# A two-layer hybrid decoder on one core: recurrent stage partly from PSUM, fewer early modulation rows, and a reordered start

## The chip, the core and the metric

The kernel runs on one core of a Trainium2 chip. The metric is the device time of one execution in microseconds (us). TensorE (PE in the profile; PEld is its weight load) multiplies matrices into eight PSUM banks; VectorE (DVE) and ScalarE (ACT) work on SBUF and PSUM; SyncE (SP) issues most of the DMA transfers, ScalarE a few.

## The reference

Two layers, 256 tokens, model width 1024. Each layer runs a half-step SwiGLU FFN, a token mixer and a second half-step FFN. The mixer of layer 0 is stick-breaking attention, that of layer 1 the Griffin RG-LRU block. Each sub-layer is RMS-normalised and takes shift, scale and gate from a conditioning vector c:

```python
mod = (c_act @ mod_w[layer] + mod_b[layer]).reshape(B, N_SUB, 3, D_MODEL)
h = rmsnorm(x, g) * (1 + scale) + shift          # sublayer_input
x = x + w * (1 + gate) * sublayer(h)

def rglru_block(h, ...):                         # D_RNN = 1280, ten blocks of 128
    gate, xb = jnp.split(h @ w_in, 2, axis=-1)
    xc = conv_b + sum of four taps of xb (a causal convolution of width 4)
    r = sigmoid(block-diagonal w_r @ xc + b_r)
    i = sigmoid(block-diagonal w_i @ xc + b_i)
    log_a = -8 * r * softplus(-lam); a = exp(log_a)
    b = sqrt(-expm1(2 * log_a)) * (i * xc)
    hs = linear recurrence h_t = a_t * h_(t-1) + b_t
    return (gelu(gate) * hs) @ w_out
```

The trunk ends with one RMSNorm.

## The kernel before

All activations lie transposed in SBUF: x is eight tiles of 128 features by 256 tokens. The weights come from HBM in float32. A chunk (`raw`) is split on the chip into a high part `wh` (ScalarE copies it to fp32r, L526) and a low part `wl` (VectorE subtracts, L529), and the activations likewise (`hx`, `arenar`). A product is then three fp32r passes on TensorE (L555): high by high, high by low, low by high. A few products run in plain float32 instead, without a split: the first chunk of the first FFN (L824), the block-diagonal gates of the recurrence (L1163), the sums of squares (L632), and the first down chunk of the recurrent stage (L572; `N32 = 1`).

The order of the work is not written by hand. Each step is recorded as an operation with an engine, a cost, its inputs and outputs; `Program.schedule` plans all of them with costs and due times (`LAT`, `START`, `SAME`), and the instructions of each engine are emitted in the planned order, which the engine then keeps. PSUM banks, weight buffers and work areas are handed out in that plan (`Buf`, `Space`).

The places that the change touches:

- `first_loads`: SP's queue loads c (`cb`), then x in two halves, then, one after the other, modulation rows and weights; ScalarE's queue loads the first parameters (`pars`). VectorE and ScalarE square x, VectorE adds the squares in pairs (L1317), and four float32 products with a matrix of ones (L632) sum them over the partitions. TensorE also runs filler products on zeros (`warm`, L1284): 4, 4 and then 18 ahead of the first real product (L824). `gbias` (L1298) is a small step on the parameters; the first modulation scales (`mf`) need it.
- `hook` and `rate`: a row of the modulation (128 outputs) is one 512 KB load and one multiply-and-sum on VectorE (L587). `rate[phase]` says how many rows are taken at each position of a phase, and `due[phase]` how many must be done near its end. Phase 0 is the first FFN, 1 attention, 2 and 3 the next two FFNs.
- `rglru`: TensorE projects xb (five pairs of 128-feature tiles); ScalarE copies a pair's halves from the bank to SBUF (`xb`); VectorE runs the four taps (`conv`, L1142 and L1145); `gates(n)` makes two float32 products per tile (L1163), two sigmoids and a tanh on ScalarE, and a product on VectorE (L1174). After the last sigmoid come, over all pairs, exponentials and squares (ScalarE) with L1220 (VectorE), square roots (ScalarE) with L1226, and the scans (L1229). Meanwhile TensorE runs the gate projections (`gate_proj`), which ScalarE copies out of their banks. Then a Gelu on ScalarE, the product y (L1236), its split (L1242), and the down projection (`down`) with five chunks of `wout`.
- Between two stages stands `residual` (x is updated, L702) and `scaled` (L650), which prepares the next stage's input.

Of the kernel before, what the change touches and what calls it, by code (L numbers as in the profile page):

```python
# [10 lines left out]
AF = mybir.ActivationFunctionType  # L11
# [358 lines left out]
def trunk(ctx, tc, xT, cb, par, modw, gu0, gu, wdn, qk, wv, wo, win, wri, wout, out):  # L370
# [111 lines left out]
    def col(off, n=1):  # L482
        return pars()[:, off : off + n]
# [644 lines left out]
    def rglru(l, s, nxt):  # L1128
        N32 = 1
        R, F = new_phase(8 * (NB - N32), 86)  # L1130
        xc, rr, th, gt, sig, wg, firsts = {}, {}, {}, {}, [], {}, []
# [3 lines left out]

        def conv(n, evict):
            xb = Buf(xbr)
            evict(n % 2, xb)
            if n % 2 == 0:
                xc[n // 2] = Buf(F, 4)  # L1140
            c, e, cs = of(xc, n)
            V(lambda: dve.tensor_scalar(c()[:, cs], xb()[:, 1 : 1 + T], col(OFF_CW + n), col(OFF_CB + n), ALU.mult,  # L1142
                                        ALU.add), T, [xb, pars], [(c, e)], ptr=2)
            for tap in range(1, 4):
                V(lambda tap=tap: dve.scalar_tensor_tensor(c()[:, cs], xb()[:, 1 + tap : 1 + tap + T],  # L1145
                                                           col(OFF_CW + tap * NR + n), c()[:, cs], ALU.mult, ALU.add), T,
                  [xb, pars, (c, e)], [(c, e)], ptr=1)

# [27 lines left out]
        def xb_proj(n2):  # L1176
            if n2 == 0:
                firsts.append(up_first((l, s), [load(win[1, i], CH, f"xb{i}") for i in range(NFIRST)]))
            if n2 < NFIRST:
                ts = next(firsts[0])  # L1180

                def evict(e, xb):
                    t, rd, c = ts[e]
                    A(lambda: xb()[:, 4:], t, AF.Identity, T, [t, rd], [xb], ptr=1, bias=c)
            else:
# [6 lines left out]
            for e in range(2):  # L1192
                conv(2 * n2 + e, evict)

        def gate_proj(n2):
            acc = Acc(f"gt{n2}")
            up(acc, load(win[0, n2], CH, f"gt{n2}"), (l, s), True)
            b = acc.b
            g = gt[n2] = Buf(F, 4)
            A(g, b, AF.Copy, 2 * T, [(b, (0, 0)), (b, (1, 0))], [g], psum=True)  # L1200

        for n2 in range(NB):
            xb_proj(n2)
            if n2 >= 2:
                gates(2 * n2 - 4)
                gates(2 * n2 - 3)
        gate_proj(0)
        for n in range(6, NR):
            gates(n)
        exps, sqs, ys = [], [], []  # L1210

        def decay(n2):
            r, t, q = rr[n2], th[n2], Buf(F, 4)
            for e in range(2):
                n, cs = 2 * n2 + e, slice(e * T, (e + 1) * T)
                exps.append(A(lambda cs=cs: r()[:, cs], lambda cs=cs: r()[:, cs], AF.Exp, T, [(r, e), nsp], [(r, e)],
                              table="exp", ptr=1, scale=lambda n=n: nsp()[:, n : n + 1], after=sig))
            A(q, r, AF.Square, 2 * T, [(r, 0), (r, 1)], [q])
            tt = [(t, 0), (t, 1)]
            V(lambda: dve.scalar_tensor_tensor(t(), q(), 1.0, t(), ALU.add, ALU.mult), 2 * T, [q] + tt, tt)  # L1220

        def scan(n2):
# [4 lines left out]
            for e in range(2):  # L1227
                cs = slice(e * T, (e + 1) * T)
                V(lambda cs=cs: dve.tensor_tensor_scan(t()[:, cs], r()[:, cs], c()[:, cs], 0.0, ALU.mult, ALU.add), T,  # L1229
                  [(c, e), (r, e)], [(t, e)])  # L1230

        def output(n2):
            g, t = gt[n2], th[n2]
            A(g, g, AF.Gelu_apprx_tanh, 2 * T, [g], [g], table="gelu", after=sqs)
            tt = [(t, 0), (t, 1)]
            V(lambda: dve.tensor_tensor(t(), t(), g(), ALU.mult), 2 * T, tt + [g], tt)  # L1236
            if n2 < N32:
# [49 lines left out]
    def first_loads(F):  # L1287
        c, b, halves = Buf(modr), [Buf(banks), Buf(banks)], []
        act_dma(lambda: pars()[:, :NP0], par[:, :NP0], [], [(pars, 0)])
        last[:] = [pr.op("DMA", 1000.0, lambda: sp.dma_start(c()[:1, :], cb), [], [c], last, lat=-900.0)]  # L1290
        warm(EARLY)
        for h in range(2):
# [4 lines left out]
        warm(MID, [pr.last_pe])  # L1297
        V(lambda: dve.scalar_tensor_tensor(gbias(), col(OFF_MB + KD, KD), 1.0, col(OFF_NG, KD), ALU.add, ALU.mult), KD,  # L1298
          [(pars, 0)], [gbias])


        pairs = []
        for h, scalar_ in enumerate(((0,), (2, 3))):
# [9 lines left out]
            for i in scalar_:  # L1313
# [100 lines left out]
```

## Time and profile before

| | us |
|---|---|
| three runs: lowest, median, highest | 959.68, 960.46, 961.25 |
| the profiled execution | 961.03 |
| its span, first to last instruction | 959.3 |
| TensorE busy | 948.8 |
| VectorE busy | 789.0 |
| ScalarE busy | 567.5 |

The profile shows one execution; its rows give the engine, the line of the kernel, the tiles written and read, the number of instructions and their time. Matmuls are pipelined, so the time of one row is longer than the distance from one to the next. A float32 product stands there as two rows. The TensorE clock that the throttle granted was 0.997 of full over the span.

### The profile page before, as it was taken

The numbers are of one execution on the slowest core, as the hardware profiler recorded it, in microseconds if no ns is written. First come the engines' busy times: TensorE is split into PE (matmuls) and PEld (weight loads), VectorE is DVE, ScalarE is ACT, GpSimd is POOL, SyncE is SP. The second block draws the span as 40 slices with busy tenths as digits, with TensorE's granted clock in tenths as the row PEclk, the third lists the DMA queues.
The fourth block names the chain that finished last, engine by engine and source line by source line (L and its number), as shares of the span: only waits on it lengthen the run. The fifth ranks groups of instructions, "written<-read, shape, count | busy, mean of one in ns | idle before, by whom it ended". The sixth has DMA issues, their size and how long they took to land.

```text
span 959.3 us, 19706 instructions
## 1 busy us (share of the span) xinstructions
PE 948.8 (99%) x8120; PEld 936.3 (98%) x8120; DVE 789.0 (82%) x1287; ACT 567.5 (59%) x925; POOL 2.4 (0%) x15
## 2 busy tenths in 40 slices
PE   9999999999999999999999999999999999999996
PEld 6999999999999999999999999999999999999996
DVE  7999988799999999888899989845997996555443
ACT  6685453379786765444466555534879785445333
POOL 1000000000000000000000000000000000000000
PEclk9999999999999999999999999999999999999998
DMA  9989999946766499889976899965243746555531
GB/s 347 405 307 373 351 353 353 334 190 249 255 222 220 180 347 366 332 297 348 363 260 255 312 345 364 355 212 198 88 173 136 264 164 235 210 182 197 169 119 44
DMA packets 48044, 251.25 MB, mean 262 GB/s; under 512 B 5457, under 2 KB 6097, under 8 KB 28242
## 3 DMA queue, kind: packets, MB, share of 16 engines
q1 hardware_dynamic: 47378, 249.43, 70.6%
q8 instruction: 63, 1.03, 0.4%
q10 hardware_dynamic: 576, 0.56, 0.2%
q14 instruction: 27, 0.22, 0.1%
HBM read 248.92 MB, written 1.05 MB: 261 GB/s over the span
## 4 chain that ended last, share of the span: by engine, by line
PE 83%; DVE 8%; ACT 3%; DMA 3%; issue 1%; SPq 0%; DVEq 0%; ACTq 0%
PE bank L555 76%; DVE wl L529 3%; DMA rawm<-in_modw 3%; PE bank L938 2%; DVE arenaf L1145 1%; PE bank L1068 1%; DVE rawm L587 1%; ACT wh L526 1%; ACT arenaf L502 1%; PE bank L572 1%; PE bank L824 1%; PE bank L632 1%; PE bank L1011 1%; DVE x L702 1%; ACT hx L502 1%
## 5 line engine op out<-in xcount | busy, mean ns | idle before, releaser
L555 PE MATMUL bank<-hx,wh 128*128 128x256 f32 (+1 forms) x3204 | 553.1, 277 | 0.8 <-DVE hx L650 0.8
L526 ACT ACTIVATE wh<-raw 128x1024 fp32r<-128x1024 f32 (+1 forms) x324 | 334.0, 1052 | 278.4 <-PE bank L555 210.1
L555 PEld LDWEIGHTS bank<-hx,wh 128*128 128x128 f32 x3204 | 485.0, 188 | 1.3 <-DVE hx L650 1.0
L529 DVE TENSOR_TENSOR wl<-raw,wh 128x1024 fp32r<-128x1024 f32 (+1 forms) x324 | 386.5, 1215 | 115.5 <-ACT wh L526 114.2
L555 PE MATMUL bank<-hx,wl 128*128 128x256 f32 (+1 forms) x1602 | 443.4, 277 | 0.0
L555 PEld LDWEIGHTS bank<-hx,wl 128*128 128x128 f32 x1602 | 301.3, 188 | 0.0
L555 PE MATMUL bank<-arenar,wh 128*128 128x256 f32 x1664 | 284.5, 277 | 0.0
L555 PEld LDWEIGHTS bank<-arenar,wh 128*128 128x128 f32 x1664 | 250.6, 188 | 0.1
L555 PE MATMUL bank<-arenar,wl 128*128 128x256 f32 x832 | 229.7, 276 | 0.0
L587 DVE SCALAR_TENSOR_TENSOR rawm<-rawm,cact 128x1024 f32<-128x1024 f32 x128 | 154.9, 1219 | 15.1 <-DMA rawm<-in_modw 15.1
L555 PEld LDWEIGHTS bank<-arenar,wl 128*128 128x128 f32 x832 | 156.2, 188 | 0.0
L502 ACT ACTIVATE arenar<-a 128x256 fp32r<-128x256 f32 x88 | 35.4, 406 | 11.5 <-DVE a L780 11.3
L502 ACT ACTIVATE sg<-bank 128x256 f32<-128x256 f32 x82 | 30.2, 370 | 17.3 <-PE bank L555 16.5
L785 DVE TENSOR_TENSOR arenar<-a,arenar 128x256 fp32r<-128x256 f32 x88 | 36.5, 419 | 0.5 <-ACT arenar L502 0.5
L780 DVE TENSOR_TENSOR a<-bank,sg 128x256 f32<-128x256 f32 x82 | 34.2, 418 | 1.8 <-ACT sg L502 1.5
L502 ACT ACTIVATE hx<-x,mf 128x256 fp32r<-128x256 f32 x40 | 18.6, 501 | 22.1 <-DVE x L702 22.0
L555 PE MATMUL bank<-hk,wh 128*128 128x256 f32 x156 | 30.3, 287 | 0.0
L702 DVE SCALAR_TENSOR_TENSOR x<-bank,mf,x 128x256 f32<-128x256 f32 x48 | 21.6, 479 | 7.7 <-PE bank L555 7.6
L938 PE MATMUL bank<-wh,hx 128*128 128x256 f32 x128 | 24.4, 285 | 0.2 <-DVE arenar L1076 0.2
L555 PEld LDWEIGHTS bank<-hk,wh 128*128 128x128 f32 x156 | 24.0, 188 | 0.3
L502 ACT ACTIVATE hx<-hpre,mf 128x256 fp32r<-128x256 f32 x41 | 19.7, 499 | 6.2 <-DVE hpre L658 6.1
L555 PE MATMUL bank<-hk,wl 128*128 128x256 f32 x78 | 21.9, 281 | 0.0
(118 smaller groups left out, 587.2 us busy)
## 6 DMA issues: line engine op xcount, KB each, us to landing
raw<-in_gu SPq DMA_DIRECT2D x79, 1024.0 KB, 5.7
rawm<-in_modw SPq DMA_DIRECT2D x128, 512.0 KB, 6.9
raw<-in_wdn SPq DMA_DIRECT2D x44, 1024.0 KB, 5.1
raw<-in_win SPq DMA_DIRECT2D x10, 1024.0 KB, 4.8
arenar<-in_modw SPq DMA_DIRECT2D x16, 512.0 KB, 9.2
raw<-in_qk SPq DMA_DIRECT2D x8, 1024.0 KB, 4.9
raw<-in_gu SPq DMA_DIRECT2D x14, 512.0 KB, 9.2
raw<-in_wout SPq DMA_DIRECT2D x5, 1024.0 KB, 5.0
```

Of the source, the lines that this page charges most:

```text
L502: act.activation(o(), i(), f, **{k: (v() if callable(v) else v) for k, v in kw.items()})
L526: act.activation(h()[:, :m], raw()[:, a : a + m], AF.Copy)
L529: dve.tensor_tensor(lo()[:, :m], raw()[:, a : a + m], f32(h()[:, :m]), ALU.subtract)
L555: pe.matmul(o(b()), wc(u()), xc(v()), start=start and n == 0, stop=stop and n == len(passes) - 1, skip_group_check=True)
L572: pr.op("PE", c_mm(n, 4), lambda: pe.matmul(o(b()), wc(w()), xc(x32()), start=start, stop=stop, skip_group_check=True), [w, x32] + ([] if ...
L587: dve.scalar_tensor_tensor(raw(), raw(), 1.0, cact(), ALU.mult, ALU.mult, accum_out=m()[:, t : t + 1])
L632: pr.op("PE", c_mm(T, 4), lambda i=i, q=q, c=c: pe.matmul(b()[:, :T], ones, q()[:, c], start=i == 0, stop=i == len(qs) - 1), [q] + [b] * ( ...
L702: dve.scalar_tensor_tensor(x[d](), acc.b()[:, j * T : (j + 1) * T], gate()[:, d : d + 1], x[d](), ALU.mult, ALU.add)
L780: V(lambda: dve.tensor_tensor(a(), b()[:, T:], sg(), ALU.mult), T, [(b, (1, 0)), sg], [a])
L785: V(lambda: dve.tensor_tensor(y[1](), a(), f32(y[0]()), ALU.subtract), n, [a, y[0]], [y[1]])
L824: pr.op("PE", c_mm(T, 4), lambda: pe.matmul(b()[:, g * T : (g + 1) * T], raw()[:, c0 : c0 + P], h0(), start=start, stop=False, skip_group_ ...
L938: pe.matmul(o, u()[:, tb * P : (tb + 1) * P], v()[:, c0 : c0 + 256], start=start and n == 0, stop=k == KD - 1 and n == 2, skip_group_check ...
```

## The change

In `first_loads` the load of c goes to ScalarE's queue, ahead of the parameters, so that x is first on SP's; the second group of squares is folded once more (three products with ones instead of four); `gbias` is planned behind that fold. The planner's start value for the DMA queue is 2900 instead of 2300.

Phase 0 takes 1.25 modulation rows per position instead of 1.5; phase 1 looks at its due number from position 8 instead of 9.

In `rglru` the last three pairs of xb stay in their PSUM bank: ScalarE computes the last tap with the bias from the bank (instead of the copy), and VectorE the other three taps from the bank, each on the columns that have a predecessor. The first two pairs are convolved on VectorE as before. The gates run three pairs behind the projection instead of two. The last two gate projections (`KEEP = 2`) stay in their banks until the Gelu reads them there. The squares of the first two pairs go to VectorE. `N32 = 0`: no down chunk is in float32; the first chunk's weights and the first pair's y are split like the others. The planner's cost of a scan is 600 ns.

```diff
-START = {"PE": 1170.0, "DVE": 2840.0, "ACT": 1960.0, "DMA": 2300.0}
+START = {"PE": 1170.0, "DVE": 2840.0, "ACT": 1960.0, "DMA": 2900.0}
...
-        N32 = 1
-        R, F = new_phase(8 * (NB - N32), 86)
+        N32 = 0
+        KEEP, TAPACT, SQACT = 2, False, (2, 3, 4)
+        R, F = new_phase(8 * (NB - N32), 86 - 4 * KEEP)
...
+            if acc is None:
+                xb = Buf(xbr)
+                evict(n % 2, xb)
+                src, rd, own = (lambda a, m: xb()[:, 4 - a : 4 - a + m]), [xb], True
+            else:
+                b, o = acc.b, (n % 2) * T
+                src, rd, own = (lambda a, m: b()[:, o : o + m]), [(b, (n % 2, 0))], False
+            if TAPACT or acc is not None:
+                A(lambda: c()[:, cs], lambda: src(0, T), AF.Identity, T, rd + [pars], [(c, e)], ptr=2, psum=acc is not None,
+                  scale=lambda: col(OFF_CW + 3 * NR + n), bias=lambda: col(OFF_CB + n))
+            else:
+                V(lambda: dve.tensor_scalar(c()[:, cs], src(0, T), col(OFF_CW + 3 * NR + n), col(OFF_CB + n), ALU.mult,
+                                            ALU.add), T, rd + [pars], [(c, e)], ptr=2)
+            for tap in range(3):
+                back = 3 - tap
+                z = 0 if own else back
+                def fn(tap=tap, back=back, z=z):
+                    u = c()[:, e * T + z : (e + 1) * T]
+                    dve.scalar_tensor_tensor(u, src(back, T - z), col(OFF_CW + tap * NR + n), u, ALU.mult, ALU.add)
+                V(fn, T, rd + [pars, (c, e)], [(c, e)], ptr=1)
...
-                def evict(e, xb):
-                    A(lambda: xb()[:, 4:], lambda: acc.b()[:, e * T : (e + 1) * T], AF.Copy, T, [(acc.b, (e, 0))], [xb],
-                      psum=True)
+                for e in range(2):
+                    conv(2 * n2 + e, acc=acc)
...
+            if n2 >= NB - KEEP:
+                gt[n2] = b
+                return
...
-            if n2 >= 2:
-                gates(2 * n2 - 4)
-                gates(2 * n2 - 3)
+            if n2 >= 3:
+                gates(2 * n2 - 6)
+                gates(2 * n2 - 5)
         gate_proj(0)
-        for n in range(6, NR):
+        for n in range(4, NR):
...
-            A(q, r, AF.Square, 2 * T, [(r, 0), (r, 1)], [q])
+            if n2 in SQACT:
+                A(q, r, AF.Square, 2 * T, [(r, 0), (r, 1)], [q])
+            else:
+                V(lambda: dve.tensor_tensor(q(), r(), r(), ALU.mult), 2 * T, [(r, 0), (r, 1)], [q])
...
-                  [(c, e), (r, e)], [(t, e)])
+                  [(c, e), (r, e)], [(t, e)], 600.0)
...
-            A(g, g, AF.Gelu_apprx_tanh, 2 * T, [g], [g], table="gelu", after=sqs)
+            if n2 >= NB - KEEP:
+                b, g = g, rr[n2]
+                rg = [(g, 0), (g, 1)]
+                A(g, b, AF.Gelu_apprx_tanh, 2 * T, [(b, (0, 0)), (b, (1, 0))], rg, table="gelu", psum=True, after=sqs)
+            else:
+                rg = [g]
+                A(g, g, AF.Gelu_apprx_tanh, 2 * T, [g], [g], table="gelu", after=sqs)
...
-        act_dma(lambda: pars()[:, :NP0], par[:, :NP0], [], [(pars, 0)])
-        last[:] = [pr.op("DMA", 1000.0, lambda: sp.dma_start(c()[:1, :], cb), [], [c], last, lat=-900.0)]
+        act_dma(lambda: c()[:1, :], cb, [], [c], 300.0)
+        act_dma(lambda: pars()[:, :NP0], par[:, :NP0], [], [(pars, 0)], 4800.0)
...
-            pairs += [(p, slice(0, T)), (p, slice(T, 2 * T))]
+            if h == 0:
+                pairs += [(p, slice(0, T)), (p, slice(T, 2 * T))]
+            else:
+                one = Buf(F, 2)
+                fold = V(lambda p=p: dve.tensor_tensor(one(), p()[:, :T], p()[:, T:], ALU.add), T, [p], [one])
+                pairs.append((one, slice(0, T)))
+        pr.op("DVE", 80.0, lambda: dve.scalar_tensor_tensor(gbias(), col(OFF_MB + KD, KD), 1.0, col(OFF_NG, KD), ALU.add,
+                                                            ALU.mult), [(pars, 0)], [gbias], [fold])
...
-    rate = {0: (1.5, SQ, 30), 1: (1.5, 0, 9), 2: (1.3, 0, 32), 3: (1.3, 0, 32)}
+    rate = {0: (1.25, SQ, 30), 1: (1.5, 0, 8), 2: (1.3, 0, 32), 3: (1.3, 0, 32)}
```

More of the change, by code (lines that the diff above doesn't have):

```diff
@@ L1141, in conv @@
             c, e, cs = of(xc, n)
[L1142 to L1147, printed above, removed]
+            if acc is None:
[18 more added lines that the diff above has]
+                V(fn, T, rd + [pars, (c, e)], [(c, e)], ptr=1)
         def gates(n):
@@ L1184, in evict @@
                     A(lambda: xb()[:, 4:], t, AF.Identity, T, [t, rd], [xb], ptr=1, bias=c)
+                for e in range(2):
+                    conv(2 * n2 + e, evict)
             else:
@@ L1187, in xb_proj @@
                 up(acc, load(win[1, n2], CH, f"xb{n2}"), (l, s), True)
-                def evict(e, xb):
-                    A(lambda: xb()[:, 4:], lambda: acc.b()[:, e * T : (e + 1) * T], AF.Copy, T, [(acc.b, (e, 0))], [xb],
-                      psum=True)
-            for e in range(2):
-                conv(2 * n2 + e, evict)
+                for e in range(2):
+                    conv(2 * n2 + e, acc=acc)
         def gate_proj(n2):
@@ L1297, in first_loads @@
         warm(MID, [pr.last_pe])
-        V(lambda: dve.scalar_tensor_tensor(gbias(), col(OFF_MB + KD, KD), 1.0, col(OFF_NG, KD), ALU.add, ALU.mult), KD,
-          [(pars, 0)], [gbias])
         pairs = []
```

6 lines of the change are left out of this document (2 added, 4 removed).

## The prediction

> **What bounds the kernel now.** I read the page first, then the table of waits of TensorE (who waited for whom, us in total, times, longest), then the chain that ended last.
>
> ```profile
> PE 948.8 (99%) x8120; PEld 936.3 (98%) x8120; DVE 789.0 (82%) x1287; ACT 567.5 (59%) x925; POOL 2.4 (0%) x15
> ...
> PE bank L555 <- DVE hx L650: 0.8, 1, 0.8
> PE bank L572 <- DVE arenaf L1236: 0.4, 1, 0.4
> PE bank L632 <- DVE arenaf L1317: 0.4, 1, 0.4
> ...
> 13.86 6.91 PE bank L824 x32
> 54.23 81.86 PE bank L555 x720
> 740.33 7.17 PE bank L572 x32
> ```
>
> TensorE is busy 948.8 of 959.3 us and its largest single waits are 0.8, 0.4 and 0.4 us. So time can be won in three ways only: fewer passes, an earlier first real product, or one of these waits. The chain gives the price of a pass. One fp32r pass takes 81.86/720 = 0.1137 us. A float32 product is recorded as two rows, and 32 rows take 6.91 us, so one product takes 2 x 0.216 = 0.432 us; the three fp32r passes that replace it take 0.341 us. VectorE or ScalarE work that is saved counts only where TensorE waits for it.
>
> **Part 1, the first microseconds.** Rows of the timeline: start, us, engine and line.
>
> ```profile
> 0.79 0.35 SPq L1290 DMA_DIRECT2D rawm<-in_cb  x1
> 1.20 0.82 SPq L495 DMA_DIRECT2D x<-in_xT  x2
> ...
> 3.30 0.16 DVE L1298 SCALAR_TENSOR_TENSOR gbias<-pars 128x8 f32<-128x8 f32 x1
> 5.78 0.96 DVE L1311 TENSOR_TENSOR arenaf<-x 128x768 f32<-128x768 f32 x1 [2.32 <-DMA x<-in_xT]
> 7.59 3.78 PE L632 MATMUL bank<-arenaf,ones 128*128 128x256 f32 x8 [0.40 <-DVE arenaf L1317]
> 8.24 0.69 DVE L1317 TENSOR_TENSOR arenaf<-arenaf 128x512 f32<-128x512 f32 x1
> 8.85 1.22 DVE L587 SCALAR_TENSOR_TENSOR arenar<-arenar,cact 128x1024 f32<-128x1024 f32 x1
> 10.00 1.22 DVE L587 SCALAR_TENSOR_TENSOR arenar<-arenar,cact 128x1024 f32<-128x1024 f32 x1
> 10.12 0.39 ACT L502 ACTIVATE mf<-mr,gbias,pars 128x1 f32<-128x1 f32 x1 [1.02 <-DVE arenar L587]
> 11.17 2.69 PE L1284 MATMUL bank<-zero 128*128 128x256 bf16 x18
> 12.43 0.48 DVE L658 SCALAR_TENSOR_TENSOR hpre<-x,mf,rst 128x256 f32<-128x256 f32 x1 [1.21 <-ACT rst L502]
> 13.01 0.51 ACT L502 ACTIVATE hpre<-hpre,mf 128x256 f32<-128x256 f32 x1 [0.43 <-DVE hpre L658]
> 13.70 7.07 PE L824 MATMUL bank<-hpre,raw 128*128 128x256 f32 x32
> ```
>
> VectorE waits 2.32 us for x. The load of c stands ahead of x on SP's queue and holds it from 0.79 to 1.20. With c on ScalarE's queue, x and every load behind it on SP start 0.41 us earlier. The bound below is 0, if x's slow arrival (issued 1.20, used 5.78) has another cause; I take 0.41, as the issue time is a plain shift. c is first on its new queue, and the parameters, now second there, are next read only behind the fold.
>
> Then, each row shifted by 0.41: the last L1317 ends at 8.52. The added fold, half as wide, lies between 0.35 (half of 0.69) and 0.48 (the 256-wide L658); with 0.45 it ends near 9.0. The two L587, 1.15 apart, end at 11.3; gbias, moved behind them in VectorE's order, adds its 0.16; mf 0.39 on ScalarE follows; L658 and the ScalarE step behind it (0.51) end near 13.05, where before they ended at 13.52. So the move of gbias eats most of what the fold gives, because mf now waits for it.
>
> On TensorE the eight L632 rows last from 7.59 to 11.17, 0.45 each. Six rows, the last two behind the fold, end near 9.9 instead of 11.17. But 18 filler matmuls (L1284) stand between them and L824.
>
> ```profile
> L632 PE MATMUL bank<-ssq,ones x12: 378/379/483, 202.5 to 950.5; 128*128 128x256 f32 x12
> L632 PE MATMUL bank<-arenaf,ones x8: 634/634/796, 7.6 to 10.7; 128*128 128x256 f32 x8
> ```
>
> The same L632 row (min/median/max ns) takes 634 ns here and 379 later: TensorE starts at a slow rate and reaches the full one only within the fillers, whose mean is 2.69/18 = 0.149 us. If that switch stays at its time and the fillers start 1.27 us earlier, 1.27 us more of slow time falls on them; at half rate that is 0.64 us of lost work, so they end at 9.9 + 2.69 + 0.64 = 13.2. L824 starts at 13.1 to 13.2 instead of 13.70: 0.55 us won. Ends of the range: 0 (no shift of x and the switch late) to 1.2 (the switch early, and mf not late). [...]
>
> **Part 2, fewer early modulation rows.** The rate 1.25 gives 36 rows (29 positions x 1.25) in place of 43 by the end of the first FFN. All 36 are used by the same date as before: 24 are due there, and 49 by the end of attention, where 48 are due, so nothing becomes late. But the 0.8 us wait at its end does not hang on their number:
>
> ```profile
> 200.01 1.22 DVE L529 TENSOR_TENSOR wl<-raw,wh 128x1024 fp32r<-128x1024 f32 x1
> 201.15 0.48 DVE L650 SCALAR_TENSOR_TENSOR hx<-x,mf,hx 128x256 fp32r<-128x256 f32 x1
> ```
>
> The last L650, for which TensorE waits, stands behind a weight split L529. In the instruction order of the changed kernel VectorE's and ScalarE's last steps before that point are the same, one modulation row among them. I take 0; at most 0.8 is won. The seven rows done later fall into FFNs where TensorE has no wait. Attention's TensorE order is the same but for six passes, so 0, within 0.5 either way.
>
> **Part 3, the recurrent stage: TensorE.** With N32 = 0 the 16 float32 products of the first down chunk become 48 fp32r passes: 16 x (0.432 - 0.341) = 1.46 us saved, with no cover needed. The chunk's weights must now be split: two wh on ScalarE, two wl on VectorE, and y of the first pair needs a hi copy and a lo subtraction. The gates of the first tiles run one projection later, in fewer blocks; this changes the order, not the number of passes.
>
> **Part 4, the recurrent stage: VectorE and ScalarE.**
>
> ```profile
> L702 DVE SCALAR_TENSOR_TENSOR x<-bank,mf,x x48: 474/478/485, 189.8 to 950.5; 128x256 f32<-128x256 f32 x48
> L1145 DVE SCALAR_TENSOR_TENSOR arenaf<-xb,pars,arenaf x30: 476/480/487, 690.1 to 712.7; 128x256 f32<-128x256 f32 x30
> ...
> ACT sg L502 <- DVE arenaf L1174: 1.5, 2, 1.0
> ...
> 723.99 0.48 ACT L502 ACTIVATE sg<-bank,pars 128x256 f32<-128x256 f32 x1
> 729.81 2.70 ACT L502 ACTIVATE arenaf<-arenaf 128x512 f32<-128x512 f32 x5
> 733.82 2.72 ACT L502 ACTIVATE arenaf<-arenaf 128x512 f32<-128x512 f32 x5
> 738.85 1.05 ACT L526 ACTIVATE wh<-raw 128x1024 fp32r<-128x1024 f32 x1
> 743.23 0.63 ACT L502 ACTIVATE arenar<-arenaf 128x512 fp32r<-128x512 f32 x1 [0.43 <-DVE arenaf L1236]
> ...
> 734.49 0.69 DVE L1226 TENSOR_TENSOR arenaf<-arenaf 128x512 f32<-128x512 f32 x1 [0.94 <-ACT arenaf L502]
> 735.21 1.27 DVE L1229 TENSOR_TENSOR_SCAN arenaf<-arenaf 128x256 f32<-128x256 f32 x2
> 736.41 0.67 DVE L1226 TENSOR_TENSOR arenaf<-arenaf 128x512 f32<-128x512 f32 x1
> 739.61 0.67 DVE L1236 TENSOR_TENSOR arenaf<-arenaf 128x512 f32<-128x512 f32 x1
> 743.11 2.36 DVE L529 TENSOR_TENSOR wl<-raw,wh 128x1024 fp32r<-128x1024 f32 x2
> 755.55 0.68 DVE L1242 TENSOR_TENSOR arenar<-arenaf,arenar 128x512 fp32r<-128x512 f32 x1
> ```
>
> Reading PSUM costs VectorE nothing: L702 reads a bank in 478 ns, the tap L1145 reads SBUF in 480. Six of the ten tiles lose their first tap on VectorE (ScalarE does it in place of the copy it did anyway). [...]
>
> Now the chain to the first down product. In before ScalarE ends the gates at 724.47, having waited 1.5 us for VectorE (sg, L1174). VectorE's lighter load and the new order take away most of that; I take 1.25 us (between 0 and 1.5). Two of the five squares go to VectorE, 2 x 0.54 us off ScalarE; but two wh of the new chunk, 0.95 us apart, stand ahead of the square roots. The roots start at 733.82 - 1.25 - 1.08 + 1.9 = 733.4, the first L1226 at 734.1, and its two pairs of scans end near 737.9. The roots (2.72), a table load and a Gelu let y of the first pair start at 738.1 and end at 738.75. ScalarE's hi copy (0.63) is done at 739.55, the lo subtraction at 740.2. Before, TensorE started at 740.33; now its first pass can start when it is ready and the second near 740.25: 0.2 us won.
>
> Then VectorE, to the last lo: 16 steps of 0.60 (L1229: two in 1.20) and 8 wl of 1.14 are 18.7 us, with gaps 759.2; before it was done at 756.23. TensorE asks for it after three chunks and 21 passes, (144 + 21) x 0.1137 = 18.8 us after 740.15, at 758.9: it waits 0.35 us. ScalarE's copies for two gate tiles (0.58 each) fall away; they stood on no path.
>
> **The sum.** -0.55 - 1.46 - 0.2 + 0.35 = -1.86 us. The profiled execution took 961.03 us around its span of 959.3 us, which makes 959.2; it lies 0.57 above the median of 960.46, so the median becomes 958.6.
>
> **The rivals.**
> *More is won* (chance 0.25): the wait for the last lo does not appear, and the start wins 1.2. For it: the sum of 18.7 us is within 0.4 of what is allowed. Against it: mf waits for gbias. Then -1.46 - 0.4 - 1.2 = -3.1, 957.4 us.
> *Only the passes are won* (0.15): the fillers run slow for longer and L824 stays near 13.6; the square-root chain keeps its old time, and y's split adds its 1.2 us to it, of which 0.2 to 0.4 is covered. Then -1.46 - 0.1 + 0.9 = -0.7, 959.8 us.
> *The recurrent tail becomes the bound* (0.10): ScalarE's sigmoids of all six late tiles come after one projection, behind banks that VectorE reads in strict order; two wh and three squares then stand in front of the roots. If the gates end at 728, 4 us later than before, the last lo comes 5.2 us later than in my sum and TensorE waits that long: -1.86 + 5.2 = +3.3, 963.8 us. It is slower than before from 1.9 us of such lateness over my sum, and over 0.2% slower from 3.8. Against it: VectorE has fewer steps ahead of the gates. [...]
>
> **How the numbers follow.** My own case has 0.50, and ranges from 957.6 to 959.5 by the ends of the start (0 to 1.2) and the waits of the tail (0 to 1). A change of 0.2% (1.9 us) is about what a measurement of this kernel can tell; 958.54 is that border, so half of my case lies on each side. Faster: 0.25 + 0.25 = 0.50; same: 0.25 + 0.15 = 0.40; slower: 0.10. The range of 8 in 10 runs from 956.9 to 960.7.
>
> **What would show it.** L572 is gone; L824 starts near 13.15; the wait for L650 near 200 us is still 0.8; the first down pass of the recurrent stage starts near 739.7 and TensorE loses some 0.4 us in its second, then some 0.35 about 19 us later; taps from a bank take 480 ns. I am wrong if the gates' last sigmoid ends after 724.5, if taps from PSUM take 540 ns, or if a new wait stands in attention.

## The result, and the profile after

The changed kernel takes **957.9 us** (median of 9 runs, 957.37 to 958.23) where the kernel before takes 960.26 in the same comparison (9 runs, 959.42 to 961.25). The ratio is 0.9978, with a 95% interval from 0.9969 to 0.9987: 1.2 to 3.0 us, or 2.1 by the ratio. The forecast was 958.6, within 956.9 to 960.7. The profiled execution took 957.58 us, its span is 955.8.

The page's first part and the table of waits of TensorE after (waited for: us in total, times, longest):

```profile
PE 946.8 (99%) x8134; PEld 935.1 (98%) x8134; DVE 793.0 (83%) x1287; ACT 568.2 (59%) x924; POOL 2.4 (0%) x15
...
PE bank L938 <- DVE arenar L1076: 0.2, 1, 0.2
PE bank L824 <- ACT hpre L502: 0.2, 1, 0.2
PE bank L632 <- ACT sq L502: 0.2, 1, 0.2
```

The three waits that the prediction named are gone: L632 for the folded squares (0.4), L572 for y (0.4), and also the 0.8 us of L555 for L650 near 200 us, which was forecast to stay. TensorE's busy time falls by 2.0 us.

The start after, in order of time for each engine (start, us, what, and in brackets the idle time before it):

```profile
0.79 0.85 SPq L495 DMA_DIRECT2D x<-in_xT  x2
...
0.79 0.51 ACTq L498 DMA_DIRECT2D rawm<-in_cb  x1
1.33 0.37 ACTq L498 DMA_DIRECT2D pars<-in_par  x1
...
10.97 0.39 ACT L502 ACTIVATE mf<-mr,gbias,pars 128x1 f32<-128x1 f32 x1
...
4.94 0.96 DVE L1335 TENSOR_TENSOR arenaf<-x 128x768 f32<-128x768 f32 x1 [1.56 <-DMA x<-in_xT]
...
8.14 0.43 DVE L1347 TENSOR_TENSOR arenaf<-arenaf 128x256 f32<-128x256 f32 x1
8.48 1.22 DVE L587 SCALAR_TENSOR_TENSOR arenar<-arenar,cact 128x1024 f32<-128x1024 f32 x1
...
10.77 0.16 DVE L1350 SCALAR_TENSOR_TENSOR gbias<-pars 128x8 f32<-128x8 f32 x1
10.90 0.42 DVE L833 TENSOR_TENSOR arenaf<-x,rst 128x256 f32<-128x256 f32 x1
11.39 0.48 DVE L658 SCALAR_TENSOR_TENSOR hpre<-x,mf,rst 128x256 f32<-128x256 f32 x1
...
12.53 7.17 PE L824 MATMUL bank<-hpre,raw 128*128 128x256 f32 x32 [0.17 <-ACT hpre L502]
19.35 0.96 PE L555 MATMUL bank<-hx,wh 128*128 128x256 f32 x2
```

x is used at 4.94 (5.78 before), the new fold takes 0.43, gbias stands behind both L587 and mf (10.97) behind gbias, as forecast. L824 starts at 12.53, 1.17 earlier than before, and not at 13.15. But the first two L555 passes behind it last 0.96 us together (0.59 before), where two such passes at 20.75 are recorded with 0.39: the second waits for hx (L848). VectorE and the weight load around it, in the kernel before and then after:

```profile
19.16 0.42 DVE L848 TENSOR_TENSOR hx<-hpre,hx 128x256 fp32r<-128x256 f32 x1 [0.35 <-ACT hpre L502]
19.51 1.22 DVE L587 SCALAR_TENSOR_TENSOR arenar<-arenar,cact 128x1024 f32<-128x1024 f32 x1
```

```profile
18.32 1.22 DVE L587 SCALAR_TENSOR_TENSOR arenar<-arenar,cact 128x1024 f32<-128x1024 f32 x1
...
19.46 0.42 DVE L848 TENSOR_TENSOR hx<-hpre,hx 128x256 fp32r<-128x256 f32 x1
...
19.93 0.19 PEld L555 LDWEIGHTS bank<-hx,wh 128*128 128x128 f32 x1 [0.41 <-DVE hx L848]
```

Before, L848 stands ahead of a modulation row (L587); in the new order it stands behind one.

The recurrent tail after (to set it beside the prediction's times add 2.19 us, by which the gates' last matmul comes earlier in this execution):

```profile
719.95 0.86 ACT L502 ACTIVATE sg<-bank,pars 128x256 f32<-128x256 f32 x2
...
722.13 4.11 ACT L502 ACTIVATE arenaf<-arenaf,nsp 128x256 f32<-128x256 f32 x10
...
731.01 2.71 ACT L502 ACTIVATE arenaf<-arenaf 128x512 f32<-128x512 f32 x5
...
735.69 0.69 DVE L1262 TENSOR_TENSOR arenaf<-arenaf 128x512 f32<-128x512 f32 x1
...
737.18 0.69 DVE L1268 TENSOR_TENSOR arenar<-arenaf,arenar 128x512 fp32r<-128x512 f32 x1 [0.20 <-ACT arenar L502]
...
756.25 0.68 DVE L1268 TENSOR_TENSOR arenar<-arenaf,arenar 128x512 fp32r<-128x512 f32 x1
```

The last sigmoid ends at 720.81 + 2.19 = 723.0 (forecast 723.2), the roots start at 733.2 (733.4), y of the first pair at 737.9 (738.1), its lo part ends at 740.1 (740.2), and the last lo ends at 759.1 (759.2). This chain was right within 0.2 us throughout. TensorE's first down pass is at 737.54, or 739.73 (739.7).

To see where the time went in all the runs below, I cut each trace at the same TensorE rows: the first L555 pass; the first product of the reciprocal root (L632) that ends the first FFN and the one that ends attention; the gates' last matmul; the first down pass of the recurrent stage; and the next L632 product. The entries are differences of the starts of these rows, in us. Every other stretch (the two middle FFNs, the last FFN, the way to the gates) is equal within 0.03 us in all fourteen profiles. The medians belong to five comparisons, in which the kernel before had 960.26 (the two first profiles), 959.7 (the three parts alone and the old rates), 959.97 (before again, c's queue, N32 = 1, taps), 959.92 (after again, gbias ahead, two squares) and 959.74 (both). The ratio and its interval are those on record; they need not be the quotient of two medians. That the last stretch is 0.27 us longer in the changed kernel's first profile than in the four other profiles of the same stage shows in no wait of its table.

| kernel | first L555 at | first FFN | attention | gates to down | gates to next root | median | ratio to before (95%) |
|---|---|---|---|---|---|---|---|
| before (first profile) | 20.42 | 182.13 | 116.31 | 22.75 | 57.47 | 960.26 | 1 |
| after (first profile) | 19.35 | 181.31 | 116.02 | 22.15 | 56.17 | 957.9 | 0.9978 (0.9969 to 0.9987) |
| before again | 20.40 | 180.94 | 116.03 | 22.73 | 57.45 | 959.7 | 0.9998 (0.9988 to 1.0007) |
| after again | 19.65 | 181.80 | 116.05 | 22.15 | 55.90 | 957.88 | 0.9979 (0.9970 to 0.9988) |
| rates alone | 20.79 | 180.94 | 116.01 | 22.62 | 57.34 | 959.3 | 0.9996 (0.9987 to 1.0005) |
| start alone | 19.77 | 181.20 | 116.05 | 22.63 | 57.35 | 958.92 | 0.9996 (0.9988 to 1.0005) |
| recurrent stage alone | 20.26 | 180.94 | 116.03 | 22.15 | 55.91 | 957.97 | 0.9986 (0.9977 to 0.9995) |
| after, old rates | 19.39 | 181.44 | 116.03 | 22.15 | 55.91 | 957.56 | 0.9983 (0.9974 to 0.9992) |
| c's queue alone | 19.65 | 182.98 | 116.03 | 22.64 | 57.36 | 961.48 | 1.0016 (1.0007 to 1.0025) |
| after, N32 = 1 | 19.80 | 180.99 | 116.05 | 22.15 | 56.76 | 958.78 | 0.9985 (0.9976 to 0.9994) |
| after, taps from SBUF | 19.56 | 181.26 | 116.00 | 24.14 | 58.22 | 961.21 | 1.0010 (1.0002 to 1.0019) |
| after, gbias ahead | 19.37 | 181.09 | 116.02 | 22.15 | 55.90 | 957.02 | 0.9970 (0.9959 to 0.9982) |
| after, two squares | 19.62 | 181.38 | 116.02 | 22.15 | 55.72 | 957.83 | 0.9975 (0.9966 to 0.9984) |
| after, both | 19.18 | 181.54 | 116.04 | 22.15 | 55.74 | 957.05 | 0.9969 (0.9957 to 0.9982) |

### The profile page after: what moved, and what is told of

Its sections match the earlier page's. It is cut to its first block, busy times and chain, and to the rows that moved or that the text cites. A ratio compares the mean times of both kernels' runs of the same rounds, so it can differ in the third digit from the quotient of the medians.

```text
span 955.8 us, 19720 instructions
## 1 busy us (share of the span) xinstructions
PE 946.8 (99%) x8134; PEld 935.1 (98%) x8134; DVE 793.0 (83%) x1287; ACT 568.2 (59%) x924; POOL 2.4 (0%) x15
## 4 chain that ended last, share of the span: by engine, by line
PE 94%; ACT 3%; DMA 2%; DVE 1%; issue 0%; SPq 0%; DVEq 0%
PE bank L555 88%; PE bank L938 2%; ACT arenaf L502 1%; PE bank L1068 1%; DMA raw<-in_gu 1%; DMA arenar<-in_modw 1%; PE bank L1011 1%; ACT wh L526 1%; PE bank L1046 1%; PE bank L1179 0%; ACT L1389 0%; PE bank L632 0%; PE bank L1048 0%; ACT arenar L502 0%; ACT sg L502 0%
## 5 line engine op out<-in xcount | busy, mean ns | idle before, releaser
L555 PE MATMUL bank<-hx,wh 128*128 128x256 f32 (+1 forms) x3204 | 553.1, 277 | 0.1
L555 PEld LDWEIGHTS bank<-hx,wh 128*128 128x128 f32 x3204 | 484.8, 188 | 0.7 <-DVE hx L848 0.4
L529 DVE TENSOR_TENSOR wl<-raw,wh 128x1024 fp32r<-128x1024 f32 (+1 forms) x326 | 388.7, 1214 | 112.6 <-ACT wh L526 111.4
L555 PE MATMUL bank<-hx,wl 128*128 128x256 f32 (+1 forms) x1602 | 443.5, 277 | 0.0
L555 PEld LDWEIGHTS bank<-hx,wl 128*128 128x128 f32 x1602 | 301.2, 188 | 0.0
L555 PE MATMUL bank<-arenar,wh 128*128 128x256 f32 x1696 | 290.6, 277 | 0.1
L555 PEld LDWEIGHTS bank<-arenar,wh 128*128 128x128 f32 x1696 | 255.6, 188 | 0.5 <-DVE arenar L1268 0.3
L555 PE MATMUL bank<-arenar,wl 128*128 128x256 f32 x848 | 234.2, 276 | 0.0
L587 DVE SCALAR_TENSOR_TENSOR rawm<-rawm,cact 128x1024 f32<-128x1024 f32 x128 | 154.8, 1218 | 15.0 <-DMA rawm<-in_modw 14.7
L555 PEld LDWEIGHTS bank<-arenar,wl 128*128 128x128 f32 x848 | 159.2, 188 | 0.0
L555 PE MATMUL bank<-hk,wh 128*128 128x256 f32 x156 | 30.2, 285 | 0.0
L555 PEld LDWEIGHTS bank<-hk,wh 128*128 128x128 f32 x156 | 23.9, 188 | 0.2
L555 PE MATMUL bank<-hk,wl 128*128 128x256 f32 x78 | 21.9, 281 | 0.0
```

Of the source, the lines that this page charges most:

```text
L529: dve.tensor_tensor(lo()[:, :m], raw()[:, a : a + m], f32(h()[:, :m]), ALU.subtract)
L555: pe.matmul(o(b()), wc(u()), xc(v()), start=start and n == 0, stop=stop and n == len(passes) - 1, skip_group_check=True)
L587: dve.scalar_tensor_tensor(raw(), raw(), 1.0, cact(), ALU.mult, ALU.mult, accum_out=m()[:, t : t + 1])
```

## The experiments

**The rates alone.** In the kernel before:

```diff
-    rate = {0: (1.5, SQ, 30), 1: (1.5, 0, 9), 2: (1.3, 0, 32), 3: (1.3, 0, 32)}
+    rate = {0: (1.25, SQ, 30), 1: (1.5, 0, 8), 2: (1.3, 0, 32), 3: (1.3, 0, 32)}
```

> The kernel before with the two new rates alone (1.25 and 8 in place of 1.5 and 9). Theory A (backlog): the wait for the last L650 near 200 us hangs on how far VectorE lags behind, and the seven early rows that are left out (some 1.2 us each on VectorE, and their loads) shorten the lag; then the 0.8 us wait is gone here, the reciprocal root that begins attention starts about 0.8 us earlier than before, and the time is 959.4 to 959.7. Theory B (the order decides, as the prediction had it, and the earlier start of the whole kernel took the wait away): the wait is still 0.8 us, and the time is that of before within 0.3 us. The start and the recurrent stage are as before by both.

The wait is gone and the first FFN takes 180.94 in place of 182.13, as theory A had it; the ratio's interval includes 1. But the wait is gone in the next three kernels too, the old rates and the old start among them, so the rates are not shown to be its cause.

**The start alone.** The kernel before with the new `first_loads` and `START`:

```diff
-START = {..., "DMA": 2300.0}
+START = {..., "DMA": 2900.0}
-        act_dma(pars ...); SP: dma_start(c)
+        act_dma(c ...); act_dma(pars ..., 4800.0)
-        gbias ahead of x's squares
+        one more fold of the second half; gbias behind it
```

> The kernel before with the edits of the start alone (c on ScalarE's queue, the added fold, gbias behind it, the planner's figure for a first load). L824 starts between 12.5 and 13.2 us, 0.5 to 1.2 earlier than before, as in the changed kernel. Theory A (backlog from 43 early rows): the 0.8 us wait for L650 near 200 us stays, and the time is 0.5 to 1.2 us under before. Theory B (the start took it away): the wait is gone, and the time is 1.3 to 2.0 us under before.

L824 starts at 12.94, within the expectation, and the wait near 200 us is gone although the modulation rows are those of before (VectorE begins 53 of them ahead of that root, as in the kernel before, and 49 with the new rates): theory A falls. Theory B isn't borne out either, because of the next kernel. The median is 0.8 us under before's 959.7, less than theory B asked, and the ratio's interval includes 1.

**The recurrent stage alone.** The kernel before with the new `rglru`:

```diff
-        N32 = 1
+        N32 = 0
+        KEEP, TAPACT, SQACT = 2, False, (2, 3, 4)
```

> The kernel before with the new recurrent stage alone. Start and first FFN as before, the 0.8 us wait near 200 us too. The 16 replaced products give 1.46 us; the down projection's first pass comes 0.6 us earlier than before relative to the gates' last matmul, as in the changed kernel, and two waits of about 0.25 us each stand in its second and its last-lo pass: 2.0 us under before after the stage, 958.2 to 958.6. By the prediction's own tail (0.2 won at the first pass, 0.35 lost later) it would be 1.3 us under before.

The stretch from the gates to the next root falls from 57.4 to 55.91, 1.5 us, between the 2.0 expected and the 1.3 of the prediction's own tail; the median is 957.97 where before has 959.7. And the wait near 200 us is gone here as well, in a kernel whose instructions up to 680 us are those of before. No edit can have removed it.

**The changed kernel with the old rates.** The rate line of the first experiment, turned back.

> The changed kernel with the two old rates (1.5 and 9). Theory A: the wait for L650 near 200 us is back with 0.4 to 0.8 us, the time is 0.4 to 1.1 us above that of the changed kernel (957.9), since 0.3 us of attention may go as well. Theory B: no wait near 200 us, and the time of the changed kernel within 0.3 us.

No wait near 200 us, and no stretch differs from the changed kernel's by more than in its own repeats. With the first experiment this settles the second part of the change: fewer early rows are worth nothing here, either way.

**The kernel before once more.** No edit.

> The kernel before, unchanged, profiled once more. The 0.8 us wait for L650 near 200 us was gone in four kernels of which one differs from before only behind 690 us. Theory C (one execution's own): the wait comes from loads that came late in the one profiled execution; then this profile shows it below 0.2 us, the first FFN takes some 181.0 us from the first L555 to the reciprocal root behind it in place of 182.1, and the span is 0.8 to 1.2 us under 959.3 less what the start differs. Theory A or B (it belongs to the kernel): 0.8 us again. The spread of the start between executions of one and the same code shows in L824: 13.4 to 14.0 by the three profiles with the old start.

Theory C holds. VectorE's timeline in this profile:

```profile
184.90 1.22 DVE L587 SCALAR_TENSOR_TENSOR rawm<-rawm,cact 128x1024 f32<-128x1024 f32 x1 [0.56 <-DMA rawm<-in_modw]
...
198.52 1.22 DVE L529 TENSOR_TENSOR wl<-raw,wh 128x1024 fp32r<-128x1024 f32 x1
199.65 0.48 DVE L650 SCALAR_TENSOR_TENSOR hx<-x,mf,hx 128x256 fp32r<-128x256 f32 x1
```

and the same row in the first profile of before:

```profile
186.39 1.23 DVE L587 SCALAR_TENSOR_TENSOR rawm<-rawm,cact 128x1024 f32<-128x1024 f32 x1 [2.24 <-DMA rawm<-in_modw]
```

The same row of the same program waited 0.56 us for its load in one execution and 2.24 in the other. The L529 and L650 that follow come 1.5 us later with it, and TensorE met that as a 0.8 us wait. Attention was 0.3 us longer in the first profile too (0.1 at its first sum of squares, 0.2 ten us behind); that this has the same cause is not shown. The span is 957.8 in place of 959.3. So of the 3.5 us between the first two spans, 1.5 are the first profile's own.

**c's queue alone.** The kernel before, gbias left where it was:

```diff
-        act_dma(lambda: pars()[:, :NP0], par[:, :NP0], [], [(pars, 0)])
-        last[:] = [pr.op("DMA", 1000.0, lambda: sp.dma_start(c()[:1, :], cb), [], [c], last, lat=-900.0)]
+        act_dma(lambda: c()[:1, :], cb, [], [c], 300.0)
+        act_dma(lambda: pars()[:, :NP0], par[:, :NP0], [], [(pars, 0)])
```

> The kernel before with c moved to the head of ScalarE's queue, the parameters second there, and gbias left at its old place ahead of the squares of x. In the changed kernel x's squares begin at 4.94 (5.78 and 6.02 with the old queue), but the parameters land 5.8 us after their issue at 1.33, where they took 1.8 us as first of the queue. Theory D (the parameters are late, and gbias had to move): VectorE waits at gbias until about 7.1, x's squares begin at 7.3, L824 starts 1.0 to 1.5 us later than before, 961 or slower. Theory E (the prediction's: the parameters are early enough and the move of gbias only costs): x's squares begin at 4.9 to 5.4 and L824 starts 0.4 to 0.8 us earlier than before, 959.

Theory D falls; theory E is right for the start and wrong for the time. x's squares begin at 5.04 and L824 at 12.82, so the queue alone gives the start's gain, and VectorE does not wait for the parameters: the planner, which counts them as landing later in second place, put gbias behind the second squares by itself. Yet the kernel is 1.5 us slower than before (interval 0.7 to 2.4): the first FFN takes 182.98. VectorE's timeline and the table of waits between 20 and 60 us:

```profile
7.32 0.16 DVE L1298 SCALAR_TENSOR_TENSOR gbias<-pars 128x8 f32<-128x8 f32 x1
...
PEld bank L555 <- DVE hx L848: 1.3, 4, 0.5
```

The list schedule came out differently in the first FFN: two modulation rows stand one behind the other ahead of each chunk's weight split, where before and after they alternate with splits, and hx of four chunks comes late. That the order changed is read from the instructions; which figure of the planner's turned it was not tried.

The DMA issues show what happens to the parameters (KB each, median us from issue to landing), before and after:

```profile
x<-in_xT SPq DMA_DIRECT2D x2, 512.0 KB, 5.0
...
pars<-in_par ACTq DMA_DIRECT2D x1, 36.0 KB, 1.8
```

```profile
x<-in_xT SPq DMA_DIRECT2D x2, 512.0 KB, 4.7
...
pars<-in_par ACTq DMA_DIRECT2D x1, 36.0 KB, 5.8
```

They land 5.8 us after their issue at 1.33, at 7.1, and x lands 0.3 us faster after its issue. The parameters are now issued behind x (1.33 against 0.79) and no longer ahead of it (0.80 against 1.20); whether that joins the two the runs don't show, as they moved both at once.

**N32 = 1 again.** The changed kernel with its first chunk as float32 products:

```diff
-        N32 = 0
+        N32 = 1
```

> The changed kernel with N32 = 1 again: the first two k steps of the recurrent down projection as 16 float32 products on the unsplit y. If a product costs 0.432 us as in the chain of before, the stage is 1.46 us longer; the first chunk needs no split of y, so the 0.27 us lost in the second pass and the 0.22 us at the last lo part of y should go: 1.0 to 1.3 us longer from the gates' last matmul to the next reciprocal root, 958.9 to 959.2 against 957.9. A rival: TensorE is bound by the chain to y and not by the passes; then the time is that of the changed kernel within 0.4 us.

The passes are the bound, not y: the products start at once behind the projections and wait for nothing. Their row in this kernel (min/median/max ns, first and last start):

```profile
L572 PE MATMUL bank<-arenaf,raw x32: 377/379/379, 737.7 to 744.4; 128*128 128x256 f32 x32
```

(744.4 - 737.7)/31 = 0.216 us a row, 0.432 a product, as the prediction had it. The stretch to the next root is 56.76, 0.85 longer than the 55.91 with N32 = 0. That is less than the 1.0 to 1.3 expected: of the 1.46 us that the cheaper passes save, 0.6 are lost again. The two waits for the split y (0.27 in the second pass, 0.22 at the last lo, none here) are 0.5 of it; 0.1 stays open. And the rest of the stage's edits, without the cheaper passes, gain 57.4 - 56.76 = 0.6.

**Taps from SBUF.** The changed kernel with the six late tiles copied first, as before:

```diff
-                for e in range(2):
-                    conv(2 * n2 + e, acc=acc)
+                def evict(e, xb):
+                    A(... xb, acc.b, AF.Copy ...)
+                for e in range(2):
+                    conv(2 * n2 + e, evict)
```

> The changed kernel with the six late convolution tiles as they were: ScalarE copies the bank to SBUF and VectorE does all four taps from there. Taps from a bank took 473 ns and from SBUF 479 in the changed kernel's profile, so the 18 taps cost the same; VectorE gets 12 first taps of 0.41 us more (ScalarE keeps its time), and the gates end up to 1.25 us later. Theory F (the tail has slack): the first down pass starts within 0.2 us of the changed kernel's and the time is 957.9 within 0.4. Theory G (the tail bounds): the first down pass comes 0.5 to 1.2 us later and the time is 958.5 to 959.1.

(It is six first taps that VectorE gets back, one for a tile, 2.4 us; the expectation counted twelve.) Theory G, and more than it asked. The gates' last sigmoid ends later, the exponentials start at 724.61 in place of 722.13 (2.3 us later as counted from the gates' last matmul, which here comes 0.14 later), and TensorE waits at the down projection: its first pass comes 2.0 us later. This kernel's waits and VectorE's taps:

```profile
PE bank L555 <- ACT arenar L502: 1.8, 1, 1.8
PE bank L555 <- DVE arenar L1272: 0.3, 1, 0.3
...
L1162 DVE SCALAR_TENSOR_TENSOR arenaf<-xb,pars,arenaf 128x256 f32<-128x256 f32 x30 | 13.4, 481 | 0.4
L1154 DVE TENSOR_SCALAR arenaf<-xb,pars 128x256 f32<-128x256 f32 x10 | 4.1, 408 | 0.7 <-ACT xb L502 0.7
```

2.3 us more in the chain cost 2.1 us of waiting and 2.3 us in the stage: the chain has next to no slack. The median is 3.3 us above the changed kernel's, which was taken in another comparison (3.1 by the two ratios); the profiled execution was near the fastest of its runs, and what the others lost besides isn't seen in it. The taps themselves cost the same from a bank as from SBUF (472 to 476 ns against 480 in the changed kernel); it is the six first taps (L1154, ten here and four after) that VectorE has more. In the changed kernel:

```profile
L1162 DVE SCALAR_TENSOR_TENSOR arenaf<-xb,pars,arenaf 128x256 f32<-128x256 f32 x12 | 5.3, 480 | 0.1
L1162 DVE SCALAR_TENSOR_TENSOR arenaf<-bank,pars,arenaf 128x253 f32<-128x253 f32 x6 | 2.8, 472 | 0.0
L1154 DVE TENSOR_SCALAR arenaf<-xb,pars 128x256 f32<-128x256 f32 x4 | 1.6, 406 | 0.0
```

What the other edits of the stage (the gates three pairs behind, the two projections kept in their banks, the squares on VectorE) give each by itself was not tried.

**The changed kernel once more.** No edit.

> The changed kernel once more, beside the kernel before on the same chip. By the stages of nine profiles the change is worth 0.9 us in the first L555 pass, of which the first FFN gives back 0.3, nothing in attention and the middle FFNs, and 1.4 in the recurrent stage: 2.0 us between profiles, and a ratio of 0.998. If the 3.4 us between the first two profiles were the change's own, it would be 0.9964 here.

957.88 against 959.92, a ratio of 0.9979: the 2.0 us that the stages add up to, not the 3.5 of the first two profiles. In this execution ScalarE waited 2.6 us for a weight load near 28 us, hx of that chunk came late and TensorE lost 0.5 us near 31 us (the first FFN takes 181.80): again one execution's own.

**gbias ahead of the rows.** The changed kernel with gbias in one step with the fold, the parameters' planned landing back at 2600, and fewer late fillers:

```diff
-EARLY, MID, LATE = 4, 4, 18
+EARLY, MID, LATE = 4, 4, 15
-                fold = V(lambda p=p: dve.tensor_tensor(one(), ...), T, [p], [one])
+                def folded(p=p):
+                    dve.tensor_tensor(one(), p()[:, :T], p()[:, T:], ALU.add)
+                    dve.scalar_tensor_tensor(gbias(), ...)
+                V(folded, T, [p, (pars, 0)], [one, gbias], cost=c_dve(T) + 80.0)
```

> The changed kernel with gbias directly behind the fold and ahead of the two L587 (one step of the planner with the fold), the planner's landing time of the parameters at its usual 2600, and 15 late fillers in place of 18. The parameters land at 7.1 and the fold ends at 8.57, so VectorE doesn't wait. mf no longer stands behind both L587: L658 waits for rst alone, and L824 starts 5.2 to 5.4 us after the first L632 (5.72 in the changed kernel); VectorE's new order has hx (L848) of the second chunk ahead of a row, which takes away the 0.3 to 0.47 us wait in the first L555 passes. Together 0.4 to 0.8 us: 957.1 to 957.5 where the changed kernel has 957.9. A rival: the second chunk's loads bound the first L555 pass, and what L824 wins is waited for there; then the reciprocal root behind the first FFN keeps its time and the whole is 957.9 within 0.3.

957.02, 0.86 us under the changed kernel's median of the same comparison; all six runs (956.62 to 957.33) lie under all eleven of the changed kernel's (957.45 to 958.39). Its timeline:

```profile
8.71 0.16 DVE L1350 SCALAR_TENSOR_TENSOR gbias<-pars 128x8 f32<-128x8 f32 x1
...
11.40 0.48 DVE L658 SCALAR_TENSOR_TENSOR hpre<-x,mf,rst 128x256 f32<-128x256 f32 x1 [0.24 <-ACT mf L502]
...
18.73 0.42 DVE L848 TENSOR_TENSOR hx<-hpre,hx 128x256 fp32r<-128x256 f32 x1
...
12.54 7.17 PE L824 MATMUL bank<-hpre,raw 128*128 128x256 f32 x32 [0.63 <-ACT hpre L502]
19.37 0.59 PE L555 MATMUL bank<-hx,wh 128*128 128x256 f32 x2
```

L824 starts 5.42 us after the first L632 (5.66 in the changed kernel's repeat), still behind mf, which ScalarE now does behind rst; and L848 comes ahead of a row, so that the first two L555 passes last 0.59 in place of 0.96 (0.84 in the repeat). By the rows some 0.2 + 0.3 us are won; the medians differ by a little more. The edit moves gbias and the number of fillers at once, and the runs don't part them: in the changed kernel's repeat the 18 fillers run from 9.94 to 13.03 and L824 waits for no step, so there the fillers hold it; here the 15 end at 11.91, and L824 waits 0.63 us for hpre.

**Two squares on ScalarE.** The changed kernel with one more square on VectorE:

```diff
-        KEEP, TAPACT, SQACT = 2, False, (2, 3, 4)
+        KEEP, TAPACT, SQACT = 2, False, (3, 4)
```

> The changed kernel with one more square of the recurrent tail on VectorE (SQACT of two tiles in place of three): ScalarE's chain to the square roots is 0.55 us shorter, VectorE gets 0.69 us more ahead of the roots, where it waits 0.97 us for ScalarE. Theory G (ScalarE's chain sets the tail, as 2.5 us more in it cost 2.0 to 2.3): y is 0.5 us earlier, the 0.27 us in the second down pass goes, and the stage from the gates' last matmul to the next reciprocal root falls from 55.9 to 56.2 to 55.5 to 55.8: 0.3 to 0.5 us. A rival: VectorE sets it, the scans come 0.2 to 0.7 later and the stage is longer by as much.

0.18 us in the stage, less than the 0.3 to 0.5 of theory G, and 0.05 in the median: the wait in the second down pass goes, and a longer one comes at the last lo part of y, where the changed kernel lost 0.22.

```profile
PEld bank L555 <- DVE arenar L1268: 0.4, 1, 0.4
PE bank L555 <- DVE arenar L1268: 0.2, 1, 0.2
```

Both theories are half right: ScalarE's chain sets the second down pass, VectorE the last lo 19 us later, so work moved from one to the other wins little.

**Both.** The last two edits together.

> The changed kernel with gbias ahead of the two L587, 15 late fillers, and two squares of the recurrent tail on ScalarE in place of three. If the two gains add, the start ends as in the kernel with gbias ahead (the reciprocal root behind the first FFN near 200.45 by x's arrival at 7.1), the stage from the gates' last matmul to the next reciprocal root takes 55.7, and the time is 956.8, a ratio of 0.9967 to before. If the last lo part of y, which came 0.2 us late with two squares on ScalarE, costs more in this order, the stage takes 55.9 and the time is 957.0.

957.05, the time of gbias ahead alone. The stage has its 55.74, but the first FFN lost 0.3 us near 30 us in this profile, behind a load for which ScalarE waited 1.9 us; a difference of 0.2 us is below what these runs can tell. This kernel and the one with gbias ahead alone are both under the kernel before by their intervals, and their medians under the changed kernel's.

## Why the prediction was right, and where it was not

**The sum.** By the stages the change is worth 0.5 us up to the end of the first FFN (the root there starts at 201.42 on average over three profiles with the old start, at 200.93 over seven with the new one; the first profile of before is left out), nothing in attention, and 1.4 us in the recurrent stage (57.4 to 56.0, the means of five and four). That is 1.9 us, against a forecast of 1.86, 2.0 by the repeat's ratio and 2.1 by the first. The terms:

**The start, -0.55: right by two errors.** The first real products come 0.9 us earlier (first L555 pass 20.47 to 19.59, the means of four and seven), not 0.55. The shift of x was mis-sized: VectorE's first square of x begins 0.86 us earlier on average (5.94 to 5.08), not 0.41, since x not only is issued 0.41 earlier but on average also lands faster (5.0 us after its issue in the kernel before and 5.2 with the recurrent stage alone, 4.7 in the changed kernel, 4.8 with c's queue alone and 5.0 with the start alone). Behind it nothing more is won: from that square to L824 it takes 7.73 us on average with the old start (7.4 to 7.9) and 7.70 with the new (7.6 to 7.9), so no gain of the fold shows, and the queue alone has L824 at 12.82. And a term was missing: behind L824 stands the second chunk's hx (L848), which does not get earlier at all (19.23 to 19.59), because a modulation row now stands ahead of it in VectorE's order. That costs 0.3 of the 0.4 us that the first FFN gives back; most of the rest is what the repeat lost near 31 us. I had named no one as late next behind L824. So the 0.55 came near the 0.5 measured by luck: one term too small, the other left out. That gbias behind the L587 holds back L824 fits the profiles in which L824 waits for hpre; where the fillers run long, they hold it. With gbias ahead and three fillers less, time was won.

The time of the fillers varied between executions. The 18 fillers in the kernel before once more, which start at the same 11.17 as in its first profile, where they took 2.69:

```profile
11.17 2.38 PE L1284 MATMUL bank<-zero 128*128 128x256 bf16 x18
```

The same code, started at the same time, took 0.3 us less; what decides it no run shows.

**Fewer early rows, 0: right, with a wrong reason beside it.** The rates are worth nothing. (By the traces VectorE begins four rows fewer ahead of that root, 49 in place of 53 with the first 16 among them, and not the seven of the working.) But "the wait for L650 near 200 is still 0.8" was wrong. The step that failed is that I took a wait from one profile for a property of the kernel. The trace showed the sign: a row ahead of it had waited 2.24 us for its load, and the profiled execution was 0.57 above the median. The median as base of the forecast kept this out of its number.

**The passes, -1.46: right** by the 0.432 us of a product; the stage keeps 0.85 of it, as N32 = 1 shows, and the waits for the split y, which the next term counts, take most of the rest.

**The tail, -0.2 and +0.35: right in kind.** The chain came within 0.2 us of every time forecast. Between the gates and the first down pass 0.5 us are won (22.67, the mean of five, to 22.15), and the second pass and the last lo lose 0.27 and 0.22 by the spacing of their starts in the changed kernel's first profile. So the forecast's -0.2, which counts the wait in the second pass, was -0.25, and its +0.35 was +0.22. With the passes that makes 1.46 + 0.5 - 0.5 = 1.46, where the stage shows 1.42 and 1.31 were forecast.

**PSUM as a source.** Taps from a bank take 472 to 476 ns (128x253 to 128x255), from SBUF 480. The 540 ns by which I would have been wrong was a mark of my own; the longest of the 18 taps from a bank took 483. To copy to SBUF first cost 2.3 us in the stage: not by the reads (481 ns a tap there), but because ScalarE's step is then the copy (0.38 us each) and VectorE has the six first taps (408 ns each). What I under-valued is how much rests on this edit: I counted the gates' end 1.25 us earlier, and without it the chain is 2.3 us later, and the stage (58.22) longer than before (57.4) in spite of the cheaper passes. The rival in which the tail becomes the bound was one edit away.

## What to carry to other kernels

Profile the kernel before twice before a single wait is priced: a wait behind a load may belong to that execution (here 2.24 us in one and 0.56 in the next), and here such waits were nearly half of the difference between the first two profiles. When a stage's start moves earlier, name the next arrival behind it, in the order of the engine that makes it; otherwise the gain is counted too high. Where a list scheduler orders the instructions, an edit of one queue can reorder a stage far away, and that can cost more than the edit wins (here c's queue alone: L824 at 12.82 in place of 13.70, and 1.5 us slower in all).

## What the runs showed of the hardware

The same 36 KB load landed 1.8 us after its issue (the kernel before) and 1.9 (the recurrent stage alone) as the first transfer of ScalarE's queue, issued at 0.80 and ahead of x's two transfers. As the second, issued at 1.33 behind a 4 KB load and behind x's, it landed 5.8 us after its issue (the changed kernel), 5.5 (the start alone) and 5.4 (c's queue alone; taps from SBUF). Whether the place in the queue or the order against x's decided it, the runs don't tell.

VectorE's step with a PSUM source ran as fast as from SBUF: 472 to 476 ns against 480, at shapes that are equal but for one to three columns.

Eighteen equal filler products at the start of the program took 2.13 us with the recurrent stage alone and 3.05 in the changed kernel with the old rates, and 2.69 and 2.38 us in two executions of the same program with the same start.
